# Eight key tiles per value-weighting block, traced two steps behind, with 11 softmax tiles and one buffer of inverses

## The chip, the cores and the metric

One NeuronCore of a Trainium2 chip runs the whole program in one launch. The metric is device time in microseconds of that core, launch included; the span of a profile runs from its first to its last recorded instruction.

## What is computed

A layer for 2048 tokens of width 1024, float32 in and out:

```
proj = x @ w_in                       # q, k, v of 8 heads A and 8 heads B (64 wide), forget gates of A
A: p = softmax(q k^T / 8 + cum[t] - cum[s], causal);  y = p v        # cum: running sum of log forget gates
B: chunks of 64, each sees itself and 8 chunks before, bias by clipped distance;  y = softmax(...) v
x1  = LayerNorm(alpha x + concat(yA, yB) @ w_out)
u   = causal depthwise conv of width 3 over (x1 @ w_up);  ffn = (value * gelu(gate)) @ w_down
out = LayerNorm(alpha x1 + ffn)
```

## The kernel before

Keys and queries are handled in chunks of 512. `attention` walks over items (p, s, c): pair of heads p (0 to 3 are heads A, 4 to 7 heads B), head s of the pair, chunk c of queries; once over chunks 0 and 1, later over chunks 2 and 3. An item is a list of key tiles of 128 keys, one step each: 4(c + 1) tiles for A; 4 for B in chunk 0 and 8 otherwise.

In one step:

- `logits` (L604) makes the logits of one key tile, transposed (keys on partitions, up to 512 queries in columns), by two matmuls into one of two PSUM banks `st` (L621, L622); VectorE adds a mask or bias where one is due (L628, L631); ScalarE takes the exponential into a tile `pt` (L633). There are PT = 10 such tiles.
- `total` (L638) adds `pt` into the item's `sums` on GpSimd (L642). There are three buffers of sums.
- `maxima` for the next item goes on: score matmuls (L584) into one of two PSUM banks `sc`, and VectorE takes maxima (L587, L592). It needs the next item's queries `qb` (L564) and keys. Its end transposes the maxima (L601) and puts them into a row of `qb` (L602).
- the generator yields, and `weave` steps the dense stream (projections for later heads, later the output projection), most of it the three matmuls of `mm3` (L187 to L189).

`weigh` (L704) multiplies the values by the softmax tiles: `y` is one PSUM bank of 128 partitions, the even tiles of a block go to its lower half of partitions and the odd ones to the upper half, so two matmuls of 64 weight columns (L708) can stand side by side in the array. Each float32 matmul is two instructions in the profile. After every GROUP = 4 tiles `weigh` is put off by LAG_P = 4 steps. After an item's last tile `close` is put off by the same lag, right behind the last `weigh`: `join` (L644) adds the two halves of `y` into `yt`; after the second head of a pair `finish` (L656) follows LAG_S = 4 steps later: two column-sum matmuls with 64 weight columns (L660), a copy into `row` (L662, two buffers), and 2 to 5 steps later four reciprocals (L666) and the multiply into `yt` (L668), which is stored for the output projection.

What is traced is not yet the order of the engines: a planner walks through the traced instructions, gives each engine the earliest traced one that it takes to be ready by its own costs, hands out buffers, and fixes each engine's order. Instructions traced later can so pass earlier ones that are blocked. On the chip each engine keeps that order.

Loads go through SP's queue in order; a key chunk is loaded as `ka`, `kb`, `vv` (five buffers of `ka` and `vv` each, L524 to L533), the queries behind them (L562 to L564). A `vv` is free when the last matmul of L708 has read it.

Of the kernel before, what the change touches and what calls it, by code (L numbers as in the profile page):

```python
# [10 lines left out]
F32 = mybir.dt.float32  # L11
# [8 lines left out]
P = 128  # L20
# [5 lines left out]
CH = 512  # L26
# [9 lines left out]
SCALE = HD ** -0.5  # L36
NEG = -1e30
LOWEST = -3e38
PT = 10
GROUP = 4  # L40
RATE1, RATE2 = 1.1, 0.6
KV, NKB, NSUM = 5, 7, 3
DLY_E = 10
VAT = (1, 0)
VPOS = (1, 0)
WFREE = 8
LAG_P = 4
HP = 1
LAG_S = 4
LAG_R = 2  # L50
# [57 lines left out]
def hymba_layer(  # L108
# [20 lines left out]
    def tl(pool, shape, dt, tag, bufs=None):  # L129
        return pool.tile(shape, dt, tag=tag, name=tag, bufs=bufs)  # L130
# [148 lines left out]
    def run_all(work):  # L279
        for _ in work:  # L280
            pass
# [225 lines left out]
    def attention(pools, chunks, ready):  # L507

        yp, pp, sm, qp, kv, ps_s, ps_t, ps_y, KB, QB = pools
# [94 lines left out]
        def logits(p, s, c, head, qs, j):  # L604

            fox = p < 4
            qa, qb = qs
            KM = MROW + 1
            ka, kb, vv = head["k", j // TQ]
            jc = j % TQ  # L610
            r = j - TQ * c
            a = max(0, r)
            b = TQ if fox else min(TQ, r + 5)
            a2, b2 = a, b
            if b - a == 1:

                a2, b2 = (a - 1, b) if a else (a, b + 1)
            w2 = slice(a2 * P, b2 * P)
            js = slice(jc * P, jc * P + P)
            st = tl(ps_t, [P, CH], F32, "st")  # L620
            nc.tensor.matmul(st[:, w2], ka[:, js], qa[:, w2], start=True, stop=False)  # L621
            nc.tensor.matmul(st[:, w2], kb[:KM, js], qb[:KM, w2], start=False, stop=True)  # L622
            w = slice(a * P, b * P)
            if not fox and r + 1 >= 0:

                t0, t1 = max(r, 0), min(r + 2, TQ)
                near = st[:, t0 * P : t1 * P]
                nc.vector.tensor_tensor(near, near, head["bt"][:, (t0 - r) * P : (t1 - r) * P], op=ALU.add)  # L628
            if fox and r >= 0:
                own = st[:, a * P : (a + 1) * P]  # L630
                nc.vector.tensor_tensor(own, own, causal_t, op=ALU.add)  # L631
            pt = tl(pp, [P, CH], F32, "pt", PT)
            nc.scalar.activation(pt[:, w], st[:, w], AF.Exp)  # L633
            if not fox and r < 0:
                nc.vector.memset(pt[0:HD, (r + 4) * P + HD : (r + 5) * P], 0.0)
            return vv[:, jc], pt, w

        def total(acc, first, pt, w):  # L638

            if first is not None and w.start:  # L640
                nc.gpsimd.tensor_copy(acc[:, : w.start], first[:, : w.start])
            nc.gpsimd.tensor_tensor(acc[:, w], (acc if first is None else first)[:, w], pt[:, w], op=ALU.add)  # L642
# [13 lines left out]
        def finish(p, c, sums, yt):  # L656

            ss = tl(ps_s, [P, CH], F32, "sc")
            for s in range(2):
                nc.tensor.matmul(ss[HD * s : HD * s + HD], ones, sums[s], start=True, stop=True)  # L660
            rs = tl(yp, [P, CH], F32, "row", 2)
            nc.scalar.activation(rs, ss, AF.Copy)  # L662

            def divide(t):
                part = rs[:, t * P : t * P + P]
                nc.vector.reciprocal(part, part)  # L666
                if t == TQ - 1:
                    nc.vector.tensor_mul(yt, rs, yt)  # L668
                    nc.sync.dma_start(y_d[p, :, c * CH : (c + 1) * CH], yt)

            for t in range(TQ):
                defer(LAG_R + t, lambda t=t: divide(t))
# [8 lines left out]
        def start(n):  # L681
            if n == len(work):
                return None, None, iter(())
            p, s, c = work[n]
            ready(p)
            if c == chunks[0]:
                head[s] = {}
                if p >= 4:
                    load_bias(head[s], 2 * p + s - 8)
                for cc in range(0 if p < 4 else max(0, c - 1), c):  # L690
                    load_keys(head[s], p, s, cc)
            load_keys(head[s], p, s, c)
            qs = []
            return head[s], qs, maxima(p, s, c, head[s], qs)

        def run_later(until):
            while later and later[0][0] <= until:
                later.pop(0)[1]()

        def defer(lag, fn):  # L700
            later.append((now + lag, fn))
            later.sort(key=lambda x: x[0])

        def weigh(y, tiles, first, last):  # L704

            for n, (v, pt, w) in enumerate(tiles):
                half = slice(HD * (n % 2), HD * (n % 2) + HD)
                nc.tensor.matmul(y[half, w], v, pt[:, w], start=first and n < 2, stop=last and n >= len(tiles) - 2)  # L708

        def close(p, s, c, y, acc):  # L710
            if s == 0:
                yts[p, c] = tl(yp, [P, CH], F32, "yt", 3)
                sums[p, c] = acc
            join(s, c, y, yts[p, c])
            if s == 1:
                defer(LAG_S, lambda: finish(p, c, (sums[p, c], acc), yts[p, c]))
# [3 lines left out]
        for i, (p, s, c) in enumerate(work):  # L720
            nhd, nqs, ahead = start(i + 1)
            if p < 4 or c == 0:
                order = list(range(TQ * c + TQ))
            else:
                order = [TQ * c - 1, TQ * c] + list(range(TQ * c - 4, TQ * c - 1)) + list(range(TQ * c + 1, TQ * c + TQ))
            acc = tl(yp, [P, CH], F32, "sums", NSUM)
            y = tl(ps_y, [P, CH], F32, "y")
            pieces = 0
            if i + 1 < len(work):
                c1 = work[i + 1][2]  # L730
                pieces = TQ * (c1 + 1 if work[i + 1][0] < 4 else min(2, c1 + 1))
            done = 0
            tiles = []
            for n, j in enumerate(order):
                run_later(now)
                tiles.append(logits(p, s, c, hd, qs, j))
                if n:
                    total(acc, tiles[0][1] if n == 1 else None, *tiles[-1][1:])
                last = n == len(order) - 1
                if len(tiles) == GROUP:  # L740
                    defer(LAG_P, lambda y=y, t=tiles, n=n, last=last: weigh(y, t, n < GROUP, last))
                    tiles = []
                if last:
                    defer(LAG_P, lambda p=p, s=s, c=c, y=y, acc=acc: close(p, s, c, y, acc))
                while done < pieces and done * len(order) < FRAC * pieces * (n + 1):
                    next(ahead, None)
                    done += 1
                now += 1
                yield (UNIT if p < 4 else UNITB) * (UC0 if c == 0 else 1.0)
            run_all(ahead)  # L750
            hd, qs = nhd, nqs
# [482 lines left out]
    with ExitStack() as st:  # L1234
# [75 lines left out]
        with ExitStack() as inner:  # L1310
            state["weights"] = prepare_weights(inner.enter_context(tc.tile_pool(name="w_s", bufs=1, side="right")))
            projected(1)
            pools = attention_pools(inner)
            weave(attention(pools, [0, 1], lambda p: projected(p // 2 + 1)), dense, RATE1)
            weave(attention(pools, [2, 3], lambda p: projected(4 + p // 2 + 1)), dense, RATE2)
# [98 lines left out]
```

## Time and profile before

| | |
|---|---|
| times of three runs | 2828.31, 2828.74, 2831.99 us |
| profiled execution | 2829.05 us, span 2827.3 us |
| TensorE busy | 2739.5 us (97%) |
| VectorE, ScalarE, GpSimd busy | 1922.9, 1174.1, 860.7 us |
| matmuls of L708 | 1088, 281.0 us busy, from 109.8 to 1348.0 us |

PE is TensorE, PEld its loading of weights, DVE VectorE, ACT ScalarE, POOL GpSimd, SP and SPq the queue that issues loads and stores. Starts of matmuls are measured, ends are modelled, so one row's duration overlaps the next row's start.

### The profile page before, as it was taken

What the parts mean: (1) busy time and instruction counts of PE and PEld (TensorE: products, weight loads), DVE (VectorE), ACT (ScalarE), POOL (GpSimd) and SP (SyncE); (2) the same over time, 40 slices, a digit from 0 to 9 for tenths busy, and PEclk for the clock granted to TensorE, in tenths of its full rate; (3) what the DMA queues carried; (4) which work ended last, traced back from release to release, by engine and by line L of the source; (5) the groups of instructions that cost most, each with busy time, mean ns of one, the idle gap of its engine ahead of it and who ended that gap; (6) DMA issues with size and microseconds to landing.
All of it is one profiled execution on the core that took longest, in us unless ns stands there. A gap on an engine that the chain in (4) does not pass through costs nothing. (4 is left out here: it accounts for less than half of the span.)

```text
span 2827.3 us, 38720 instructions
## 1 busy us (share of the span) xinstructions
PE 2739.5 (97%) x12632; PEld 2046.1 (72%) x12632; DVE 1922.9 (68%) x3415; ACT 1174.1 (42%) x2033; POOL 860.7 (30%) x916
## 2 busy tenths in 40 slices
PE   8899999999999999999997999999999999999998
PEld 7675757676666666766785877788877788888886
DVE  4456566777667755668569888876558777777548
ACT  4434344444444444424225555553222544554222
POOL 2234332426547556334115222221011211110012
PEclk9999999999999999999998999999999999999999
DMA  7675667766455545677883444428779222226964
GB/s 238 188 209 185 207 179 227 207 202 196 135 168 186 167 124 154 194 209 219 289 318 131 138 156 154 156 90 292 268 229 327 82 87 81 79 80 210 318 222 161
DMA packets 324618, 527.40 MB, mean 187 GB/s; under 512 B 70688, under 2 KB 86176, under 8 KB 324416
## 3 DMA queue, kind: packets, MB, share of 16 engines
q1 hardware_dynamic: 324416, 524.93, 58.2%
q8 instruction: 100, 1.64, 0.3%
q14 instruction: 102, 0.84, 0.1%
HBM read 362.65 MB, written 162.14 MB: 186 GB/s over the span
## 5 line engine op out<-in xcount | busy, mean ns | idle before, releaser
L187 PE MATMUL acc<-slot,slot 128*128 128x512 f32 (+2 forms) x3128 | 1188.5, 380 | 35.2 <-ACT slot L180 26.4
L189 PE MATMUL acc<-slot,slot 128*128 128x512 f32 (+2 forms) x3128 | 1183.6, 379 | 12.8 <-DVE slot L183 11.8
L188 PE MATMUL acc<-slot,slot 128*128 128x512 f32 (+2 forms) x3128 | 1182.6, 378 | 0.1
L180 ACT ACTIVATE slot<-slot 128x512 fp32r<-128x512 f32 (+1 forms) x688 | 415.9, 623 | 730.0 <-DVE slot L1138 161.5
L187 PEld LDWEIGHTS acc<-slot,slot 128*128 128x128 f32 x3128 | 594.4, 190 | 161.1 <-ACT slot L180 31.8
L189 PEld LDWEIGHTS acc<-slot,slot 128*128 128x128 f32 x3128 | 593.2, 190 | 136.7 <-DVE slot L183 18.2
L188 PEld LDWEIGHTS acc<-slot,slot 128*128 128x128 f32 x3128 | 594.4, 190 | 113.5 <-issue 3.6
L183 DVE TENSOR_TENSOR slot<-slot,slot 128x512 fp32r<-128x512 f32 (+1 forms) x570 | 432.1, 769 | 251.5 <-ACT slot L180 222.8
L642 POOL TENSOR_TENSOR sums<-sums,pt 128x512 f32<-128x512 f32 (+3 forms) x416 | 421.3, 1013 | 238.7 <-ACT pt L633 182.5
L633 ACT ACTIVATE pt<-st 128x512 f32<-128x512 f32 (+3 forms) x544 | 262.4, 493 | 332.3 <-PE st L622 120.2
L708 PE MATMUL y<-pt,vv 128*64 128x512 f32 (+3 forms) x1088 | 281.0, 506 | 0.5 <-DVE yt L650 0.5
L183 POOL TENSOR_TENSOR slot<-slot,slot 128x512 fp32r<-128x512 f32 (+1 forms) x122 | 168.0, 1378 | 274.5 <-ACT slot L180 193.2
L621 PE MATMUL st<-qa,ka 128*128 128x512 f32 (+2 forms) x544 | 208.8, 386 | 8.3 <-ACT pt L633 8.2
L584 PE MATMUL sc<-kb,qb 66*128 66x512 f32 (+2 forms) x544 | 187.0, 373 | 12.8 <-DMA qb<-qh_d 4.4
L622 PE MATMUL st<-qb,kb 97*128 97x512 f32 (+2 forms) x544 | 189.9, 357 | 3.4 <-ACT qb L602 3.0
L587 DVE TENSOR_REDUCE mx<-sc 128x1 f32<-128x512 f32 x192 | 127.8, 685 | 74.7 <-PE sc L584 73.5
L621 PEld LDWEIGHTS st<-qa,ka 128*128 128x128 f32 x544 | 102.3, 189 | 98.7 <-issue 45.4
L708 PEld LDWEIGHTS y<-pt,vv 128*64 128x64 f32 x1088 | 81.6, 136 | 121.6 <-issue 106.4
L584 PEld LDWEIGHTS sc<-kb,qb 66*128 66x128 f32 x544 | 98.7, 189 | 84.6 <-DVE mx L592 19.2
L642 POOL TENSOR_TENSOR sums<-pt 128x384 f32<-128x384 f32 (+1 forms) x64 | 78.9, 1233 | 249.8 <-PE sc L660 160.3
L870 DVE SCALAR_TENSOR_TENSOR v<-u,cw,v 128x1024 f32<-128x1024 f32 x88 | 115.0, 1307 | 58.4 <-ACT v L869 58.2
L592 DVE CUSTOM_DVE_ANT_0 junk<-sc,bq 128x512 bf16<-128x512 f32 (+2 forms) x224 | 108.3, 483 | 45.5 <-PE sc L584 37.0
(113 smaller groups left out, 2259.6 us busy)
## 6 DMA issues: line engine op xcount, KB each, us to landing
slot<-wd_d SPq DMA_DIRECT2D x308, 256.0 KB
slot<-in_w_up_dram SPq DMA_DIRECT2D x176, 256.0 KB
wd_d<-w_hl SPq DMA_DIRECT2D x77, 512.0 KB
slot<-wo_d SPq DMA_DIRECT2D x128, 256.0 KB
h_d<-v SPq DMA_DIRECT2D x44, 512.0 KB
slot<-h_d SPq DMA_DIRECT2D x88, 256.0 KB
slot<-in_w_qk_dram SPq DMA_DIRECT2D x66, 256.0 KB
xq_d<-slot SPq DMA_DIRECT2D x56, 256.0 KB
```

Source lines behind the costliest of these rows:

```text
L180: nc.scalar.activation(hi, src, AF.Copy)
L183: lo_eng.tensor_tensor(lo, src, f32(hi), op=ALU.subtract)
L187: nc.tensor.matmul(acc, wh, mh, start=first, stop=False, **more)
L188: nc.tensor.matmul(acc, wh, ml, start=False, stop=False, **more)
L189: nc.tensor.matmul(acc, wl, mh, start=False, stop=last, **more)
L584: nc.tensor.matmul(sc[:, m0:m1], qb[:KR, tq], kb[:KR, m0:m1], start=True, stop=True)
L587: nc.vector.tensor_reduce(m, sc[:, k0:k1], axis=AX.X, op=ALU.max)
L621: nc.tensor.matmul(st[:, w2], ka[:, js], qa[:, w2], start=True, stop=False)
L622: nc.tensor.matmul(st[:, w2], kb[:KM, js], qb[:KM, w2], start=False, stop=True)
L633: nc.scalar.activation(pt[:, w], st[:, w], AF.Exp)
L642: nc.gpsimd.tensor_tensor(acc[:, w], (acc if first is None else first)[:, w], pt[:, w], op=ALU.add)
L708: nc.tensor.matmul(y[half, w], v, pt[:, w], start=first and n < 2, stop=last and n >= len(tiles) - 2)
```

## The change

A block of `weigh` takes eight tiles, or what is left at an item's end; it and `close` are put off by two steps; there are 11 tiles `pt` and one buffer `row`. A tile `pt` and a buffer `row` are of one size.

```diff
-PT = 10
-GROUP = 4
+PT = 11
+GROUP = 8
...
-LAG_P = 4
+LAG_P = 2
...
-            rs = tl(yp, [P, CH], F32, "row", 2)
+            rs = tl(yp, [P, CH], F32, "row", 1)
...
-                if len(tiles) == GROUP:
+                if len(tiles) == GROUP or last:
                     defer(LAG_P, lambda y=y, t=tiles, n=n, last=last: weigh(y, t, n < GROUP, last))
                     tiles = []
```

## Rows read from the trace of the kernel before

**Rows 1.** Page of the profile: span, busy time of TensorE, one group of section 5.
```profile
span 2827.3 us, 38720 instructions
PE 2739.5 (97%) x12632; PEld 2046.1 (72%) x12632; DVE 1922.9 (68%) x3415; ACT 1174.1 (42%) x2033; POOL 860.7 (30%) x916
...
L587 DVE TENSOR_REDUCE mx<-sc 128x1 f32<-128x512 f32 x192 | 127.8, 685 | 74.7 <-PE sc L584 73.5
```
**Rows 2.** Windows (last: L708): PE, PEld, DVE, ACT, POOL busy; clock, DMA, GB/s.
```profile
105.00:1352.00 1247.00, 1217.27 (x6033) 821.83 (x6031) 809.81 (x1935) 530.72 (x1049) 562.79 (x591) 1.00 0.62 187
...
1352.00:2827.00 1475.00, 1434.01 (x6157) 1152.09 (x6156) 1067.17 (x1373) 601.40 (x910) 280.51 (x290) 0.99 0.55 184
...
105.00:1352.00 1247.00, 281.01 (x1088) 81.60 (x1088) 1.00 0.62 187
```
**Rows 3.** Timeline of TensorE, a whole block: start, us, operation, count [idle before].
```profile
852.67 0.40 PE L189 MATMUL acc<-slot,slot 128*128 128x512 f32 x1
853.00 1.94 PE L708 MATMUL y<-pt,vv 128*64 128x512 f32 x8
854.86 0.50 PE L621 MATMUL st<-qa,ka 128*128 128x512 f32 x1
855.20 0.40 PE L622 MATMUL st<-qb,kb 97*128 97x512 f32 x1
```
**Rows 4.** Waits, 105 to 1352 us: who waited for what: us, times, longest.
```profile
POOL sums L642 <- PE sc L660: 160.3, 20, 27.7
...
PEld y L708 <- issue: 106.4, 387, 0.6
...
PEld sc L584 <- DMA qb<-qh_d: 14.8, 17, 2.7
...
ACT pt L633 <- POOL sums L642: 10.2, 10, 2.6
...
PE st L621 <- ACT pt L633: 8.0, 11, 2.2
...
PE sc L660 <- DVE mx L592: 0.3, 1, 0.3
```
**Rows 5.** Timeline of TensorE behind an item's border: logits, a cut block, scores.
```profile
749.79 0.44 PE L621 MATMUL st<-qa,ka 128*128 128x512 f32 x1
...
753.03 0.28 PE L189 MATMUL acc<-slot,slot 128*128 128x256 f32 x1
753.24 1.07 PE L708 MATMUL y<-pt,vv 128*64 128x512 f32 x2
754.99 0.73 PE L584 MATMUL sc<-kb,qb 66*128 66x512 f32 x2 [0.68 <-DMA qb<-qh_d]
755.65 1.08 PE L708 MATMUL y<-pt,vv 128*64 128x384 f32 x6
756.66 0.50 PE L621 MATMUL st<-qa,ka 128*128 128x512 f32 x1
757.00 0.40 PE L584 MATMUL sc<-kb,qb 66*128 66x512 f32 x1
```
**Rows 6.** Timeline of TensorE: the first block, and the last two with sums.
```profile
109.79 1.50 PE L708 MATMUL y<-pt,vv 128*64 128x512 f32 x8
...
1343.64 1.08 PE L660 MATMUL sc<-sums,ones 128*64 128x512 f32 x4
1344.55 1.46 PE L708 MATMUL y<-pt,vv 128*64 128x512 f32 x8
...
1347.08 1.29 PE L708 MATMUL y<-pt,vv 128*64 128x384 f32 x8
```
**Rows 7.** Timelines of VectorE and ScalarE: last multiply and copy of inverses.
```profile
1350.01 0.95 DVE L668 TENSOR_TENSOR yt<-row,yt 128x512 f32<-128x512 f32 x1
...
1352.43 0.60 ACT L662 ACTIVATE row<-sc 128x512 f32<-128x512 f32 x1 [3.40 <-PE sc L660]
```
**Rows 8.** Waits of SP's queue in the same stretch.
```profile
SPq L533 <- PE y L708: 46.6, 24, 4.7
```

## The prediction

> **What bounds the kernel now.** Read the busy table first: TensorE is busy for 2739.5 of 2827.3 us [rows 1]. The windows show where the change can act: 105 to 1352 us holds all 1088 matmuls of the line that weighs the values (L708); the 1475 us behind it hold none, and their instructions stay as they are [rows 2]. In the attention stretch the granted clock is 1.00 (2.4 GHz), and TensorE is busy for 1217.3 of 1247 us, VectorE 809.8, GpSimd 562.8, ScalarE 530.7. So TensorE sets the end, and dense work (projections, output projection) fills what attention leaves.
>
> Busy does not mean at peak: ends of matmuls are modelled, so I go by starts. A 512-column matmul of the dense lines starts 0.23 us after the one before. An uncut weighing block of four full tiles (8 instructions, two per tile) starts at 853.00. Two of them, on either half of the columns, run side by side: 512 columns in 0.42 us (four of the like at 1343.64 give way after 0.91 us [rows 6]), 1.69 us for the block. From the last dense start (852.67) to the second start behind the block (855.20) is 2.53 us; less 0.23, 1.69 and 0.23 that is 0.38 us for changing from 128 columns of weights to 64 and back [rows 3]. Over all whole blocks this comes to 0.36 us. It is told by the starts: the weight loads of L708 show 106.4 us of idle time, 387 times, that no engine caused [rows 4].
>
> Second, blocks get cut. The four tiles are traced in one go, but what stands on TensorE is ordered by trace position and by what the planner holds to be ready. A score matmul (L584) traced earlier that was blocked slips in as soon as it is ready. At 753.24 one tile stands alone, then two scores (which waited 0.68 us for qb's load), then the other three tiles [rows 5]. From the last dense start (753.03) to the second start behind the block (757.00) is 3.97 us; nominal are 0.12 + 2 x 0.23 + 1.28 + 0.23 = 2.09 and the wait is 0.68, so 1.20 us is overhead, 0.84 more than uncut: the cut adds a change of width, and it falls between the two tiles of a pair, which then no longer run side by side.
>
> I followed the timeline of TensorE through the stretch from the first block to the last [rows 6]. 136 blocks make 230 runs of L708: 67 whole, 44 in two pieces, 25 in three or more, so 94 cuts, 93 of them between partners. The sum of overhead over the blocks is 121 us: 136 x 0.36 = 49, and 72 for cuts, 0.77 us each. This is the pool that the change draws from.
>
> **The change, part by part.**
> 1. *Fewer blocks.* Tiles per query chunk are 4, 8, 12 or 16 in the forgetting heads and 4 or 8 in the chunked ones. By four that is 136 blocks; by eight, with a rest of four, 80: six for each of 8 forgetting heads (1 + 1 + 2 + 2) and four for each of 8 others. The matmuls stay 1088. 56 x 0.36 = 20 us less.
> 2. *Where cuts fall.* A block is now traced two steps behind its last tile: at step 9 of its own item, or at step 1 of the next. Against the order of the kernel before, I counted the score matmuls that would be traced earlier but still unissued there. At step 9 (16 blocks, only in items of 12 or 16 tiles) it is 0 or 1; at step 1 (64 blocks) mostly 1 to 3, because scores of the next item wait for qb, whose load is issued behind the border: the logits of step 0 start at 749.79, the scores at 754.99 [rows 5]. The block stood at step 3, 3.45 us behind step 0; at step 1 it would start near 751 and, twice as long, end near 755: just when scores come free. I take 1.1 cuts for each of the 40 long border blocks, 0.4 for the 24 short ones, 0.2 at step 9, and 8 more by logits: 44 + 10 + 3 + 8 = 65. At 0.77 that is 50 us instead of 72. Bounds: 30 cuts (scores come after the blocks; 23 us) and 2 per border block (136; 105 us).
> 3. *Sums.* The two column-sum matmuls of `finish` (L660) are 64 wide too. Now they fall at step 7 of the following item, beside a weighing block, and share its change: 22 of 32 times, as at 1343.64 [rows 6]. With both lags counted they fall at step 5, beside a block only where that item has four tiles. I count 16 more lone groups x 0.36 = 6 us (0 if the planner pulls them together).
> 4. *Earlier close.* Joining, finishing and dividing move two steps forward. GpSimd waits 160.3 us, 20 times, for L660 to free a buffer of sums; ScalarE waits for those sums 10.2 us, 10 times, since GpSimd then holds softmax tiles; TensorE waits 8.0 us for ScalarE's tiles [rows 4]. Two steps are about 4 us of each GpSimd wait. Worth 0 to 8 us on TensorE; I take 3.
> 5. *Eleven tiles kept.* When a block was traced, 7 of 10 tiles were held; now 9 of 11. The exponentials after the block have two free tiles instead of three. Behind a blocked exponential stand ScalarE's copies for the dense work, and TensorE behind these. Lower bound 0 (the block stands ahead of the logits that fill those two); upper: 0.5 us at each of 64 border blocks, 32 us, a little under the 0.73 us mean of TensorE's 11 waits for these tiles. I take 3, nearest to the 8.0 us row. The Trainium skill, Perfetto Trace Analysis, section Optimization Strategy, warns that a gap that repeats on the busiest engine can mean too few buffers in SBUF or PSUM for the next tile; by that rule the sum would take the upper end and the gain would vanish. No run here shows it: the repeated gap at L708 has no releaser, so I keep 3.
> 6. *One buffer of inverses.* The copy into `row` (L662) must wait for the multiply of the chunk before (L668). The closest pair I find is the last: multiply over at 1350.96, next copy at 1352.43, so 1.5 us to spare [rows 7]; elsewhere it is 2.3 us or more. Zero; bounded by a wait of 1 us at 32 places. Queued behind it would be exponentials.
> 7. *Values' loads.* SP waits 46.6 us, 24 times, for L708 to free a vv tile [rows 8], and qb's load stands behind it in SP's order. The first tiles of an item are released two steps later, its last ones two steps earlier. Zero, plus or minus 5 us.
> 8. *Long blocks.* 3.7 us in which TensorE feeds neither ScalarE nor VectorE. VectorE is at 65% of the stretch, so it catches up, but scores pile up behind it. Hidden by dense work; what isn't is in the share below.
>
> Sum on TensorE: after 29 + 50 + 6 = 85 us against 121, so 36 less; plus 3, minus 3. A quarter to a third of that I expect back as waits on VectorE and loads, as TensorE already has 28 us of named waits in the stretch (11 rows, the first and the last in [rows 4]) and its order is fixed by a plan, not by what is ready on the chip: 36 x 0.7 = 25 us. The profiled execution took 2829.05 us around a span of 2827.3; 2829.05 - 25 = 2804. The median of the runs shown is 0.3 us lower, which is nothing here.
>
> **Rivals.**
> *Blocks stay whole* (30 cuts): 121 - 29 - 23 - 6 = 63 less, 0.8 of it on the end: 2779. For it: no cut in the sixteen blocks in the middle of 16-tile items now. Against: the border.
> *Saved, then waited*: the blocks are fewer but VectorE's scores, two free softmax tiles and SP's order give back most of it: 0 to 14 us off, about 2822. For it: the share of VectorE and the 14.8 us that weight loads of scores wait for qb [rows 4]. Against: dense work is there to fill in.
> *Cut at the border* (slower): scores of the next item come ready during the long block, two at first, then one per 0.69 us as VectorE clears banks [rows 1]. Two cuts in each of 64 border blocks and 8 more are 136: 29 + 105 + 6 = 140, 19 us more than now, plus a little idle: 2850. It decides from (121 - 29 - 6) / 0.77 = 112 cuts, 1.6 per border block. For it: blocks with scores pending are in three pieces 25 times now, though short. Against: the short blocks and the early start.
> *The planner undoes it*: tiles pulled ahead as they come ready, so that eight traced together stand as four and four: about 120 to 136 pieces before cuts; within 0.2%.
>
> **How the numbers follow.** Forecast (15 to 40 us off) 0.45; whole blocks 0.13; saved and waited 0.22, a little under half of it over 0.2% faster; cut at the border 0.17; undone 0.03. 0.2% is 5.7 us, about what can be told from no change. Faster: 0.45 + 0.13 + 0.10 = 0.68; same: 0.12 + 0.03 = 0.15; slower 0.17. The range reaches from whole blocks, 2779, to the lower part of the border case, 2838; the forecast's own is 2789 to 2814.
>
> **What would show it.** Right: in the timeline of TensorE 80 blocks in 130 to 165 runs of L708, most uncut blocks x16, idle time of L708's weight loads down from 106 us to about 75, the stretch to about 1352 shorter by 20 to 30 us, and the rest unchanged. Parts 5 and 7: waits of ScalarE's exponentials and of SP for L708 no longer than now. Wrong: more than 112 cuts; or runs down as said and TensorE's named waits up by as much; or a gain behind the attention stretch.

## The result and the profile after

The changed kernel took 2806.39, 2810.02 and 2812.15 us in three executions; its ratio to the kernel before is 0.9926, 95% interval 0.9911 to 0.9941. Run again (e0_after, six executions, median 2812.97 us) the ratio is 0.9943, 0.9925 to 0.9961. So it is 16 to 21 us faster; 25 were forecast. One execution of the changed kernel (12939.83 us, granted clock 0.16 from 505 us on), one of e8 (6664.28 us) and one of e11 (2921.24 us) are left out, and all lines "after" are of the profile of e0_after (execution 2813.71 us, span 2811.9).

Page and windows after (columns as in [rows 1, 2]; the last line is L708 alone):
```profile
span 2811.9 us, 38705 instructions
PE 2718.5 (97%) x12632; PEld 2050.0 (73%) x12632; DVE 1917.2 (68%) x3415; ACT 1174.9 (42%) x2033; POOL 858.1 (31%) x916
```
```profile
105.00:1352.00 1247.00, 1214.45 (x6098) 840.38 (x6096) 809.55 (x1947) 534.70 (x1055) 561.16 (x597) 0.99 0.62 189
...
1342.00:2811.00 1469.00, 1427.12 (x6146) 1146.23 (x6143) 1065.97 (x1370) 600.13 (x908) 280.81 (x290) 0.99 0.55 185
...
105.00:1352.00 1247.00, 258.89 (x1088) 86.29 (x1088) 0.99 0.62 189
```
Busy shares hardly moved: TensorE still reads 97%. What moved is L708: the same 1088 matmuls, 281.0 us busy before, 258.9 now. Of the 15.4 us between the two spans, 10 came out of the attention stretch: from the first 64-column matmul to the last, 109.8 to 1351.8 before, is 107.3 to 1339.3 now. 2.5 us came ahead of it (with the shorter lag alone, in e2, the first of these matmuls stands at 106.5) and 2.9 behind it, where nothing was changed. Over before, e0_after and the experiments whose profiles are used here, the part behind takes 1470.6 to 1475.5 us and the stretch 1178.6 to 1277.0: what the experiments move lies in the stretch.

Timeline of TensorE after: a whole block of eight, then a group of sums that stands alone, then a block at an item's border (start, us, operation, count). They answer to [rows 3], [rows 6] and [rows 5].
```profile
745.65 0.28 PE L189 MATMUL acc<-slot,slot 128*128 128x256 f32 x1
745.86 3.65 PE L708 MATMUL y<-pt,vv 128*64 128x512 f32 x16
749.44 0.50 PE L621 MATMUL st<-qa,ka 128*128 128x512 f32 x1
749.78 0.40 PE L622 MATMUL st<-qb,kb 97*128 97x512 f32 x1
```
```profile
739.21 0.40 PE L189 MATMUL acc<-slot,slot 128*128 128x512 f32 x1
739.53 1.08 PE L660 MATMUL sc<-sums,ones 128*64 128x512 f32 x4
740.54 0.50 PE L621 MATMUL st<-qa,ka 128*128 128x512 f32 x1
740.88 0.40 PE L622 MATMUL st<-qb,kb 97*128 97x512 f32 x1
```
```profile
758.06 0.40 PE L601 MATMUL sc<-ident_r,nm 128*1 128x128 f32 x4
758.30 0.49 PE L621 MATMUL st<-qa,ka 128*128 128x512 f32 x1
...
758.86 0.28 PE L189 MATMUL acc<-slot,slot 128*128 128x256 f32 x1
759.07 1.07 PE L708 MATMUL y<-pt,vv 128*64 128x512 f32 x2
760.07 0.50 PE L622 MATMUL st<-qb,kb 97*128 97x512 f32 x1
760.50 2.79 PE L708 MATMUL y<-pt,vv 128*64 128x512 f32 x14
763.23 0.50 PE L621 MATMUL st<-qa,ka 128*128 128x512 f32 x1
763.57 0.63 PE L584 MATMUL sc<-kb,qb 66*128 66x512 f32 x2
```
The whole block: 749.78 - 745.65 = 4.13 us, less 0.12 and 0.23 for the dense matmul and the logits and 3.39 for eight tiles, leaves 0.39 us. Eight tiles pay what four paid. The lone sums: 740.88 - 739.21 = 1.67, less 0.23 + 0.85 + 0.23, leaves 0.36: the same price, which beside a block was shared. The border block was cut, but not by scores: these came only behind it (763.57), as step 2 had it. It was cut by the second logits matmul of step 0 (L622), which needs the maxima that L601 was just transposing.

Waits after, 105 to 1352 us, for [rows 4] and [rows 8] (us, times, longest):
```profile
POOL sums L642 <- PE sc L660: 153.4, 17, 33.8
PEld y L708 <- issue: 95.0, 348, 0.7
...
PEld st L622 <- ACT qb L602: 20.1, 30, 2.0
PE st L621 <- ACT pt L633: 14.2, 16, 3.1
ACT pt L633 <- POOL sums L642: 9.8, 8, 3.4
PEld sc L584 <- DMA qb<-qh_d: 7.2, 10, 1.1
...
PE st L622 <- ACT qb L602: 6.9, 10, 1.7
```
```profile
SPq L533 <- PE y L708: 42.6, 37, 2.5
```
Before, the weight loads of L622 waited less for the row of maxima:
```profile
PEld st L622 <- ACT qb L602: 8.4, 16, 1.8
```
Idle weight loads of L708 fell by 11 us (I had looked for 30). This row does not follow the changes of width: it is 88.4 us in e10, where 80 blocks stand uncut, and in e6, which has the most runs of all (343), it is
```profile
PEld y L708 <- issue: 72.8, 240, 0.4
```
TensorE waits longer for softmax tiles (8.0 to 14.2 us). The waits for qb's load went from 14.8 to 7.2 us.

Following TensorE through the stretch and summing block by block: the overhead of L708 (time beyond paired matmuls, the price of each change of width, of cuts, and waits inside blocks) was 136.5 us before and is 100.9 us after, 36 less. Lone sums took back 7. The starts of all other matmuls, beyond what they nominally take, lost 59 us before and 77 after, 18 more: logits 11, dense lines 6. That is where half of the saving went.

A part of these 18 us is the clock. In the stretch the granted clock stood at 0.50 (1.2 GHz) for 10.2 us before, in three pieces, and for 23.9 us after, in four; six of the seven pieces came during, or within some 2 us after, a wait of TensorE of 1.4 to 3.1 us. One piece of before, then one of after with its wait ahead of it:
```profile
784.50:787.90 3.40, 3.40 (x13) 3.01 (x12) 1.59 (x4) 0.92 (x2) 1.28 (x1) 0.50 0.35 112
```
```profile
618.60:625.40 6.80, 6.23 (x18) 4.95 (x19) 5.63 (x18) 2.52 (x4) 0.00 (x0) 0.50 0.60 189
```
```profile
618.14 0.45 PE L584 MATMUL sc<-kb,qb 66*128 66x384 f32 x1 [1.41 <-DVE mx L592]
...
619.55 0.63 PE L187 MATMUL acc<-slot,slot 128*128 128x512 f32 x1
619.97 0.63 PE L188 MATMUL acc<-slot,slot 128*128 128x512 f32 x1
```
There a 512-column matmul starts 0.42 us after the one before, not 0.23. Some 4 of the 18 us lie in these pieces, an estimate from the starts in them.

### The profile page after: what moved, and what is told of

It is laid out like the page before. It is cut to its first block, busy times and chain, and to the rows that moved or that the text cites. A ratio compares the mean times of both kernels' runs of the same rounds, so it can differ in the third digit from the quotient of the medians.

```text
span 12938.0 us, 38705 instructions
## 1 busy us (share of the span) xinstructions
PE 12898.7 (100%) x12632; PEld 8568.3 (66%) x12632; DVE 1903.4 (15%) x3415; ACT 1192.3 (9%) x2033; POOL 805.0 (6%) x916
## 4 chain that ended last, share of the span: by engine, by line
PE 99%; DMA 1%; issue 0%; DVE 0%; ACT 0%; SPq 0%; POOLq 0%; POOL 0%; ACTq 0%; DVEq 0%
PE acc L187 26%; PE acc L189 26%; PE acc L188 26%; PE y L708 8%; PE st L621 4%; PE sc L584 4%; PE st L622 4%; PE sc L660 1%; PE acc L855 1%; PE sc L601 0%; DMA slot<-in_xT_dram 0%; DMA slot<-in_w_qk_dram 0%; DMA w_raw<-in_w_out_dram 0%; DMA kl_d<-slot 0%; DMA wd_d<-w_hl 0%
## 5 line engine op out<-in xcount | busy, mean ns | idle before, releaser
L187 PE MATMUL acc<-slot,slot 128*128 128x512 f32 (+2 forms) x3128 | 4435.0, 1418 | 18.3 <-ACT slot L180 17.8
L189 PE MATMUL acc<-slot,slot 128*128 128x512 f32 (+2 forms) x3128 | 4427.1, 1416 | 0.0
L188 PE MATMUL acc<-slot,slot 128*128 128x512 f32 (+2 forms) x3128 | 4427.1, 1416 | 0.0
L187 PEld LDWEIGHTS acc<-slot,slot 128*128 128x128 f32 x3128 | 2480.7, 793 | 984.4 <-issue 948.5
L189 PEld LDWEIGHTS acc<-slot,slot 128*128 128x128 f32 x3128 | 2483.6, 794 | 970.6 <-issue 886.2
L188 PEld LDWEIGHTS acc<-slot,slot 128*128 128x128 f32 x3128 | 2479.2, 793 | 948.3 <-issue 936.2
L708 PE MATMUL y<-pt,vv 128*64 128x512 f32 (+3 forms) x1088 | 1054.9, 1885 | 0.0
L621 PE MATMUL st<-qa,ka 128*128 128x512 f32 (+2 forms) x544 | 652.8, 1201 | 9.0 <-ACT pt L633 9.0
L708 PEld LDWEIGHTS y<-pt,vv 128*64 128x64 f32 x1088 | 240.5, 363 | 611.2 <-issue 605.9
L622 PE MATMUL st<-qb,kb 97*128 97x512 f32 (+2 forms) x544 | 624.2, 1156 | 1.3 <-ACT qb L602 1.3
L584 PE MATMUL sc<-kb,qb 66*128 66x512 f32 (+2 forms) x544 | 608.8, 1167 | 1.7 <-DMA qb<-qh_d 0.9
L621 PEld LDWEIGHTS st<-qa,ka 128*128 128x128 f32 x544 | 376.2, 692 | 314.3 <-issue 278.7
L584 PEld LDWEIGHTS sc<-kb,qb 66*128 66x128 f32 x544 | 375.8, 701 | 245.0 <-issue 213.4
L622 PEld LDWEIGHTS st<-qb,kb 97*128 97x128 f32 x544 | 395.4, 728 | 138.8 <-issue 128.2
```

Of the source, the lines that this page charges most:

```text
L187: nc.tensor.matmul(acc, wh, mh, start=first, stop=False, **more)
L188: nc.tensor.matmul(acc, wh, ml, start=False, stop=False, **more)
L189: nc.tensor.matmul(acc, wl, mh, start=False, stop=last, **more)
L584: nc.tensor.matmul(sc[:, m0:m1], qb[:KR, tq], kb[:KR, m0:m1], start=True, stop=True)
```

## The experiments

Theory: the time goes with the changes of width and the cuts, each at its price. Rivals: only the number of blocks counts and a cut is a sign of a wait that is there anyway; or the earlier close and the eleventh tile did it; or what is saved comes back as waits. Runs and cuts are counted in the order that the planner fixed (sums, of the same width, do not part a run). *Priced* is 0.36 us for each block and lone group of sums and 0.77 us for each cut, against 125 us of before; *measured* is the ratio's distance from 1, on 2829 us, with its interval.

| kernel | blocks | cuts | lone sums | priced | measured us | ratio |
|---|---|---|---|---|---|---|
| before | 136 | 94 | 10 | 0 | 0 | 1 |
| e0_after | 80 | 97 | 29 | -11 | -16 (-21 to -11) | 0.9943 |
| e1, eight, lag 4 | 80 | 118 | 26 | +4 | -2 (-5 to +2) | 0.9994 |
| e2, lag 2 alone | 136 | 94 | 12 | +1 | -6 (-8 to -3) | 0.9980 |
| e3, 11 tiles, one `row` | 136 | 97 | 11 | +3 | +5 (+2 to +9) | 1.0019 |
| e4, scores from step 3 | 80 | 86 | 34 | -18 | -14 (-19 to -10) | 0.9950 |
| e6, blocks of two | 272 | 71 | 7 | +30 | +32 (+27 to +36) | 1.0112 |
| e7, eight tied, lag 2 | 80 | 54 | 30 | -44 | -42 (-48 to -36) | 0.9851 |
| e8, four tied, lag 4 | 136 | 21 | 12 | -55 | -38 (-44 to -32) | 0.9866 |
| e9, eight tied, lag 3 | 80 | 44 | 24 | -54 | -53 (-58 to -47) | 0.9814 |
| e11, eight whole, lag 2 | 80 | 0 | 31 | -85 | -59 (-65 to -52) | 0.9792 |
| e12, four whole, lag 4 | 136 | 0 | 13 | -71 | -50 (-56 to -44) | 0.9824 |
| e10, eight whole, lag 3 | 80 | 0 | 29 | -86 | -71 (-78 to -64) | 0.9748 |

**e0_after: the changed kernel again.**

> The changed kernel again, for a profile at full clock. In its planned order the 80 blocks stand in 177 runs of L708 (97 cuts; 94 before) and 29 groups of L660 stand alone (10 before). Widths and cuts (0.36 us a block and a lone group, 0.77 us a cut): 29 + 75 + 10 = 114 us of overhead against 125, so 11 us less at most, 2818. Blocks alone decide, cuts are a sign of waits and cost nothing of their own: 56 x 0.36 = 20 us less, 2810. Earlier close and more tiles held decide: TensorE's waits for ScalarE's tiles (8.0 us) and GpSimd's for L660 (160 us) fall, and the overhead at L708 stays.

Measured 2812.97 us. Between the two prices. TensorE's waits for tiles rose, and GpSimd's for L660 fell little (160.3 to 153.4 us), which speaks against the earlier close as the cause; no run moves `close` without `weigh`.

**e1_group8_lag4: eight without the shorter lag.**
```diff
-LAG_P = 2
+LAG_P = 4
```


> Blocks of eight, 11 tiles and one buffer of inverses, but traced four steps behind as before: all 11 tiles are held when a block is due. 198 runs of L708 (118 cuts), 26 lone groups of L660. Widths and cuts: 29 + 91 + 9 = 129 us against 125: 2825 to 2835, no gain from eight alone. Blocks alone decide: 20 us less, 2810. Earlier close decides: as before, 2830, plus waits of exponentials for tiles.

Measured 2825.17 us, no difference from before. Twenty microseconds of fewer blocks were there and 24 more cuts took them. Blocks alone do not decide. The changed kernel differs from this one in the lag alone: with 21 cuts fewer and three lone groups more it is 14 us faster (15 by the price).

**e2_lag2 and e3_tiles11: the other two parts alone.**
```diff
-LAG_P = 4
+LAG_P = 2
```


> The kernel before with the shorter lag alone: blocks of four, 10 tiles, two buffers of inverses, traced two steps behind. 136 blocks in 230 runs (94 cuts, as before), 12 lone groups of L660. Widths and cuts: the same 125 us, so 2825 to 2832. Earlier close decides: most of the change's 15 to 19 us, 2810 to 2815, and GpSimd's waits for L660 down.


```diff
-PT = 10
+PT = 11
...
-            rs = tl(yp, [P, CH], F32, "row", 2)
+            rs = tl(yp, [P, CH], F32, "row", 1)
```


> The kernel before with 11 softmax tiles and one buffer of inverses alone; blocks of four and the lag stay. 233 runs (97 cuts), 11 lone groups. Widths and cuts: 128 against 125, so 2828 to 2833. One buffer of inverses costs: ScalarE's copies into row wait for VectorE, 2835 or more. The eleventh tile gives: waits of exponentials for GpSimd's sums fall, 2820 to 2825.

The lag alone gave 6 us (median 2823.35) with as many cuts, outside of both expectations; by its timeline the overhead of L708 fell by 8 us (136.5 to 128.2), as 79 blocks stood whole instead of 67 and others were cut more often. GpSimd's wait for L660 fell only from 160.3 to 150.3 us. Eleven tiles and one buffer of inverses alone cost 5 us (2836.15), of which the price explains 3. That is the time forecast for one buffer that costs, but the reason given there is not in the trace: no copy into `row` waits for VectorE.

**e6_group2: the price of a block.**
```diff
-GROUP = 4
+GROUP = 2
```


> The kernel before with blocks of two: 272 blocks in 343 runs (71 cuts), 7 lone groups. Widths and cuts: 98 + 55 + 3 = 156 us, 31 more than before: 2845 to 2858 (half to all of it on the end). Blocks cost nothing of their own (only cuts do): 23 fewer cuts, so 2810 to 2820.

Measured 2860.36 us, 32 more (2 us above the range), though it has 23 fewer cuts. A change of width has a price of its own, and all of it reached the end.

**e4_scores2: no scores ahead of the border block.**
```diff
-                while done < pieces and done * len(order) < FRAC * pieces * (n + 1):
+                while n >= 2 and done < pieces and done * len(order) < FRAC * pieces * (n + 1):
```


> The changed kernel, but the scores of the next item are traced only from the third step of an item on, so none stands ahead of the border block. 166 runs (86 cuts), 34 lone groups. Widths and cuts: 29 + 66 + 12 = 107 us, 7 less than the changed kernel: about 2808. Scores at the border are the cause of the cuts: should have fallen to a few tens; the plan says no, so other things cut there. Maxima finish later: logits of the next item wait longer for the row of maxima in qb, 2815 or more.

Measured 2813.59 us, as the changed kernel, with 86 cuts instead of 97. Scores ahead of the block are not what cuts most blocks now.

**e7_after_glued and e8_before_glued: most cuts taken away.** Each matmul of a block but the first gets the highest priority and an edge that keeps it behind the one before it; the edge orders the engine's queue and waits for nothing. The planner orders all the rest anew around the tied blocks.
```diff
...
-                nc.tensor.matmul(y[half, w], v, pt[:, w], start=first and n < 2, stop=last and n >= len(tiles) - 2)
+                with tc.high_priority() if n else ExitStack():
+                    m = nc.tensor.matmul(y[half, w], v, pt[:, w], start=first and n < 2, stop=last and n >= len(tiles) - 2)
+                if n:
+                    tc.add_manual_dep(m.ins, before.ins.name, BEHIND, reason="block")
+                before = m
```


> The changed kernel with each block's matmuls behind the first tied together: each goes right behind the one before it if its tile is ready, before anything traced earlier. 134 runs of L708 (54 cuts instead of 97), 30 lone groups. Widths and cuts: 29 + 42 + 11 = 81 us, 33 less than the changed kernel: 2777 to 2790 if most of it reaches the end. Blocks alone decide: as the changed kernel, 2810 (80 blocks in both). Saved, then waited: fewer cuts but TensorE waits for scores' banks, about 2810 or above, with the waits of L584 for L587 and L592 up.

> The kernel before (blocks of four, four steps behind) with the same tie: 157 runs (21 cuts instead of 94), 12 lone groups. Widths and cuts: 49 + 16 + 4 = 70 us, 55 less than before, thus less than the changed kernel: 2775 to 2795. Blocks alone decide: as before, 2830. Saved, then waited: about 2825, with waits of TensorE up by what the cuts gave.

Measured 2786.76 and 2791.32 us. The first differs from the changed kernel by 43 cuts and one lone group, and is 26 us faster; the second is the kernel before with 73 fewer cuts, 38 us faster, and beats the change with blocks of four. Taking cuts away gave 26 us for 43 and 38 us for 73: 0.5 to 0.6 us each at the end, less than the 0.77 us on TensorE. A cut costs time of its own.

**e9, e10, e11, e12: fewer cuts still, then none.** e9 is e7 with LAG_P = 3. In the other three the first matmul of a block also waits until the softmax tiles of its whole block are written (`logits` hands on its last write of a tile as `x[3]`):
```diff
...
+                else:
+                    for x in tiles:
+                        tc.add_manual_dep(m.ins, x[3].ins.name, READY, reason="block")
```


> The tied blocks of eight, traced three steps behind instead of two: 124 runs (44 cuts instead of 54), 24 lone groups instead of 30; 10 of 11 tiles are held when a block is due. Widths and cuts: 29 + 34 + 9 = 72 us, 9 less than tied at two steps: 2778 to 2787. Two free tiles were already few: waits of TensorE and ScalarE for tiles go up, 2787 or more.

> Blocks of eight traced three steps behind, tied as in e9, and in addition the first matmul of a block waits until all its tiles are there: 80 blocks in 80 runs, no cut, 29 lone groups of L660. Widths and cuts: 29 + 0 + 10 = 39 us, 86 less than before: 2745 to 2765. Saved, then waited: blocks that start later hold tiles and push scores back, so no faster than tied alone (2775), with TensorE's waits for tiles and for scores' banks up.

> The changed kernel with whole blocks (no cut instead of 97) and nothing else: 80 runs, 31 lone groups. Widths and cuts: 29 + 11 = 40 us, 74 less than the changed kernel: 2740 to 2765. Cuts only show waits that are there anyway: as the changed kernel, 2812.

> The kernel before with whole blocks (no cut instead of 94) and nothing else: 136 runs, 13 lone groups. Widths and cuts: 49 + 5 = 54 us, 71 less than before: 2758 to 2780, some 15 us slower than whole blocks of eight. Cuts only show waits: 2829. If blocks of eight cost by starving VectorE and ScalarE, this one is as fast as whole blocks of eight or faster.

Measured 2775.14 (e9, 3 us below its range), 2759.62 (e10, within), 2773.78 (e11, 9 us above) and 2780.41 us (e12, at its upper end). Here is one and the same block in the timeline of the changed kernel, and then in e10 (where `weigh` is L711, the logits L623 and L624, the scores L586):
```profile
222.46 0.40 PE L584 MATMUL sc<-kb,qb 66*128 66x512 f32 x1
222.78 1.07 PE L708 MATMUL y<-pt,vv 128*64 128x512 f32 x2
223.79 0.39 PE L621 MATMUL st<-qa,ka 128*128 128x256 f32 x1
224.01 0.28 PE L622 MATMUL st<-qb,kb 97*128 97x256 f32 x1
224.22 1.08 PE L708 MATMUL y<-pt,vv 128*64 128x512 f32 x4
225.23 0.39 PE L621 MATMUL st<-qa,ka 128*128 128x256 f32 x1
225.46 0.28 PE L622 MATMUL st<-qb,kb 97*128 97x256 f32 x1
225.58 0.39 PE L621 MATMUL st<-qa,ka 128*128 128x512 f32 x1
225.90 1.08 PE L708 MATMUL y<-pt,vv 128*64 128x512 f32 x4
226.91 0.40 PE L601 MATMUL sc<-ident_r,nm 128*1 128x128 f32 x4
227.24 1.08 PE L708 MATMUL y<-pt,vv 128*64 128x384 f32 x6
228.25 0.44 PE L621 MATMUL st<-qa,ka 128*128 128x384 f32 x1
```
```profile
223.17 0.34 PE L624 MATMUL st<-qb,kb 97*128 97x384 f32 x1
223.44 3.22 PE L711 MATMUL y<-pt,vv 128*64 128x512 f32 x16
226.59 0.62 PE L586 MATMUL sc<-kb,qb 66*128 66x512 f32 x2
```
In the first, the block lies in four pieces of one, two, two and three tiles, and TensorE changes width eight times; in the second twice. The first tile, alone on half of the array, takes as long as the two of the next piece: 1.01 us from start to next start. The four pieces take 4 x 1.01 = 4.0 us, the whole block 3.15.

Not all that is priced comes back: at no cut 71 of 86 us (e10), 59 of 85 (e11) and 50 of 71 (e12). Followed start by start as above, to within a few us, L708 and the lone sums take 96, 90 and 72 us less than before, and the starts of all other matmuls lose 32, 39 and 21 us more; the stretch is 63, 48 and 51 us shorter. The clock has a part in it (0.50 for 27.3 us of the stretch in e10 and in e11, for 10.2 in e12). The waits of e10 show another:
```profile
PE st L623 <- ACT pt L635: 18.8, 18, 2.7
PE sc L586 <- DVE mx L594: 5.0, 4, 2.1
PE sc L586 <- DVE mx L589: 3.9, 6, 2.1
...
PEld y L711 <- issue: 88.4, 313, 0.7
```
TensorE's named waits in the stretch, summed over this view, are 27.6 us before, 31.7 in the changed kernel, 37.1 in e10 and 48.0 in e11. Whole blocks two steps behind wait for their last tile, as e11 shows in a row that is 0.9 us in e10:
```profile
PEld y L711 <- ACT pt L635: 9.6, 20, 1.4
```
One step more is worth 14 us (e10 against e11), though it holds one tile more. The best of all, e10, is 70 us faster than before by its medians and 53 us faster than the change.

## Why the prediction was right, and where it was off

The direction and the mechanism were right: changes of width became fewer, and the attention stretch grew shorter. The place was right for two thirds of the time; 5.4 us of 15.4 lie ahead of the stretch and behind it, where none was forecast. The time was 2810 to 2813 (medians) for a forecast of 2804 (own range 2789 to 2814). That it fell into this range is in part luck: of the signs named for it, the runs of L708 (177, not 130 to 165), the idle weight loads (95.0 us, not about 75) and the stretch (10 us shorter, not 20 to 30) did not come.

1. *Fewer blocks*: right. 80 blocks, 0.36 to 0.39 us each, 20 us less; e6 shows the price from the other side.
2. *Where cuts fall*: this step failed. I put 65 cuts; there are 97 in the planned order, where before had 94 (taken block by block it is 97 in both: three times before, a piece of one block ran straight on into another block). The part on scores held: cuts with nothing but scores in them fell from 52 to 27, and the border block shown above ends before the scores come. But I allowed 8 cuts for logits. At the border the logits wait for the maxima's row, the block is begun meanwhile, and logits, transposes and dense lines cut it as they come ready: logits stand in 53 of the 97 cuts. That the block is begun as filler, for want of earlier work, is my reading of the order and was not tested. Counted by place, heads A in chunks 2 and 3 went from 29 to 14 cuts and heads B there from 27 to 23; in chunks 0 and 1 heads A went from 16 to 31 and heads B from 25 to 29. Why there is open; it is not for want of dense work (2.8 dense matmuls per us in that part of the timeline after, 2.1 in chunks 2 and 3). e4 confirms that scores are not the main part: with none traced ahead, 74 of its 86 cuts hold something else than scores alone. The term was -22 us; the timelines give -9 (0.83 us a cut before, 0.74 after, with less waiting for qb's load inside), and another 7 for waits inside whole blocks. With the 20 of step 1 these are the 36 us.
3. *Sums*: right in kind. 19 more lone groups where I had 16; 0.36 us each in the timeline.
4. and 5. *Earlier close, eleven tiles*: I took 3 us off and 3 on. GpSimd's wait for L660 fell by 7 us of 160, not by 4 us a time, and ScalarE's for the sums by 0.4: in these rows the close gave next to nothing. TensorE's wait for ScalarE's tiles rose by 6.2 us (8.0 to 14.2), where I took 3, far from the upper end of 32. That tiles held are the reason is not shown: e2, which holds fewer than before, has 11.6 us in that row, and e3, which has one free tile more, 6.1. The Trainium skill, Perfetto Trace Analysis, section Optimization Strategy, says that a gap which repeats on the engine that should be full can mean too little SBUF or PSUM for the next tile. The trace agrees in sign only, by these 6.2 us.
6. *One buffer of inverses*: the closest pair of multiply and next copy after is 2.0 us apart, so nothing waits there. The 5 us of e3 are not explained by it; what the price leaves of them, some 2 us, stays open, within its interval.
7. *Loads*: SP's waits for L708 went from 46.6 to 42.6 us; zero was right.
8. *The share that reaches the end*: I took 0.7 of 36. My 36 already held the sums; 29 were found (36 less 7), and 16 to 21 of them arrived, 0.55 to 0.72; in the stretch itself it was 10, the rest of the 29 standing at logits and dense lines. With 0.7 the 29 give 20: the seven less on TensorE, mainly from step 2, are 5 us of the 4 to 9 that are missing to 25. That the share was too high is not sure. I put all of it down to waits; a lower clock, of which I had no term, was part of it.

The idle weight loads, by which I had seen the change of width told as well, do not tell it (e6 and e10 above); the starts do.

Of the rivals, "saved, then waited" holds in part; "cut at the border" is real in place and price but not in number, 97 against the 112 that would have turned the sign; e1, with 118, lost the whole gain. "The planner undoes it" is real in kind: 81 of the 177 runs hold one tile (97 of 233 pieces before), but the time moved by 0.6 to 0.7%, not within its 0.2%.

## What to carry to other kernels

Where narrow matmuls share the array with wide ones, count the runs in the planned order, not the groups in the source: each run costs a change of width, and a run that ends between two partners of a pair costs their running side by side as well. Making groups longer gains little while a planner may cut them; tying a group together, and letting it start only when all of it is ready, gave more than doubling its length (four whole -50 us, eight cut -16 us). The two together gave -59 us at the lag of the change, and -71 with one step more of lag, without which the group waits for its own last tile.

## What the runs showed that was not expected

A tile weighed alone takes 1.01 us from start to start, as long as two side by side in a piece of their own. A 64-column matmul pays the same 0.36 us for entering and leaving whether it is a group of four instructions (L660) or of sixteen (L708). And scores, which I held to be the ones that cut, make 27 of the 97 cuts alone: at the border shown it is the logits of the next item that come ready in the middle of the block. Making the groups whole also leaves TensorE more waits elsewhere: starts of the other matmuls lose 21 to 39 us more, part of it at half the clock.
